# Head sums in two float32r products, with their buffers in the spare columns up to the inverse

## The chip, the cores and the metric

The kernel runs on one NeuronCore of one Trainium2 chip. The metric is the device time of one execution in microseconds (us); lower is better.

## The reference, cut to what matters

A two-layer decoder trunk on x of 512 tokens by 1024 features. Layer 0 mixes tokens by RWKV-7 (8 heads of 64, a state updated along the tokens) and by stick-breaking attention (8 heads of 64); layer 1 by a gated linear recurrence; each is followed by a mixture of 16 experts. The change touches layer 0 only, where four quantities are summed over the 64 features of a head:

```python
kk = heads(k * k_k)
kk = kk / jnp.maximum(jnp.sqrt(jnp.sum(kk * kk, axis=-1, keepdims=True)), 1e-12)
...
bonus = jnp.sum(r_h * k_h * r_k.astype(f32), axis=-1, keepdims=True) * v_h
...
q = rmsnorm(heads(p[..., :B_WIDTH]), q_norm_g)
k = rmsnorm(heads(p[..., B_WIDTH:2 * B_WIDTH]), k_norm_g)
```

The state recurrence is computed in chunks of 64 tokens; that needs the inverse of a triangular 64 by 64 matrix for each head and chunk, before any step of the recurrence.

## The kernel before, in words

Features lie on the 128 partitions and tokens along the free axis, so two heads (a pair) share a tile of 128x512, and a sum over a head's 64 features is a matrix product with a 128x128 matrix of ones in two diagonal blocks: `bo` (ones) and `bo64` (ones divided by 64). Both are float32, as is the operand. All large products instead use float32r operands, cut into a rounded high part and a remainder (`split`: a copy on ScalarE, L297, and a subtraction on VectorE, L298), with three products for a full one (L325 to L327).

Layer 0 runs in this order. `lora` makes the decays. `pair(p)`, four times, projects k, r and v of two heads (three projections of 24 products each, `shifted` and `proj_fm`; L338 and L339 take the result out of PSUM), sums over heads twice (the product on L435, used by L436; the one on L450, used by L451) and builds the chunk operands; `chunks` multiplies them (L483, masked on L489; L493 transposes). `qkv(p)`, four times, projects q, k and v of the attention; q and k are squared (L695), summed over heads (L697) and normalised (L698, L699 on ScalarE, L700 on VectorE, which also frees the projection's bank); v is transposed (L709). Then `inverse` inverts the 32x32 diagonal blocks of all chunks at once on VectorE: a transpose (L507) into `Z`, a ladder of 31 multiply and reduce pairs (L513, L514) that read `Z`, two transposes back (L515, and L520 into `TT`), and copies on ScalarE (L517). Small TensorE products complete the 64x64 inverse (L531, L540, taken out on L533 and L542). `values` prepares the values (L562 to L582). After that the recurrence steps and the attention run interleaved in an order written out by hand (z, a1, a2, a3, d1 and so on of `attend`; p1 to a4 of `step`), then the output projection and the experts.

Outside the hand-ordered part, each engine's order is set when the kernel is built, from the program's order and from when operands are expected to be ready. An engine works through its own list in that order, and waits at the head of it.

There are two projection banks in PSUM (`pj`), so a projection can start when the result of the one before last has been taken out. Memory on chip is handed out by an arena of columns; a request takes the free stretch with the least room that fits, and an address reused is waited for:

```python
fit = [(min(o + s, hi) - max(o, lo), max(o, lo)) for o, s in self.free_list]
fit = [f for f in fit if f[0] >= n]
...
return self.take(min(fit)[1], n)
```

Beside the main tile A of 38336 columns there is a spare stretch of 2560 columns (tile S, `self.more`), float32 in layer 0, which `swap` remakes as float32r or float32 later by closing its pool and opening another in the same place.

Of the kernel before, what the change touches and what calls it, by code (L numbers as in the profile page):

```python
# [8 lines left out]
F32 = mybir.dt.float32  # L9
F32R = mybir.dt.float32r  # L10
# [8 lines left out]
T = 512  # L19
D = 1024  # L20
# [13 lines left out]
SCOLS = 2560  # L34
# [2 lines left out]
P0, P1 = 7, 7  # L37
LOW = 6584
MID = LOW + 3 * 2048
WO0 = [LOW + D * i for i in range(5)] + [20152 + D * i for i in range(3)]  # L40
WO1 = LOW + 7056
FLY = 5
QQ = 3
# [116 lines left out]
class Kern:  # L160
# [180 lines left out]
    def consts_even(self):  # L341
        nc, ar = self.nc, self.ar

        self.bo = ar.get(128)
        self.bo64 = ar.get(128)
        for b, v in ((self.bo, 1.0), (self.bo64, 1.0 / 64)):
            nc.gpsimd.memset(b.f(), 0.0)
            for s in range(2):
                nc.gpsimd.memset(b.f()[s * 64:s * 64 + 64, s * 64:s * 64 + 64], v)

        self.cm = ar.get(128)
        nc.gpsimd.memset(self.cm.f(), 1.0)
        for s in range(2):
            v = self.cm.f()[s * 64:s * 64 + 64]
            nc.gpsimd.affine_select(v[:, 0:64], v[:, 0:64], [[1, 64]], OP.is_gt, 0.0, base=0, channel_multiplier=-1)
            nc.gpsimd.affine_select(v[:, 64:128], v[:, 64:128], [[1, 64]], OP.is_ge, 0.0, base=0, channel_multiplier=-1)

        self.atc = ar.get(128)
        self.identb, self.late = self.atc.b(2, 128)[:, 0], self.atc.b(2, 128)[:, 1]
        nc.gpsimd.tensor_copy(self.identb, self.ident)  # L360
        nc.gpsimd.memset(self.late, 0.0)
        nc.gpsimd.affine_select(self.late, self.late, [[-1, 128]], OP.is_gt, -FAR, base=0, channel_multiplier=1)

        self.sm = ar.get(T)
        nc.gpsimd.memset(self.sm.f(), 1.0)
        nc.gpsimd.memset(self.sm.f(8, 64)[:, :, 0:1], 0.0)

    def lora(self):
        nc, ar, I = self.nc, self.ar, self.I
        self.L1, self.G1, self.G2 = ar.get(T), ar.get(T), ar.get(T)  # L370

        du = ar.get(T)
        dv, q = du.f(), [slice(s * 64, s * 64 + 64) for s in range(2)]
        for s, name in enumerate(("decay_up", "iclr_up")):
            nc.sync.dma_start(dv[q[s]], I[name][0])
        sig = []
        self.shifted(LORA, self.L1.f())
        sig.append(nc.scalar.activation(self.L1.f()[0:64], self.L1.f()[0:64], AF.Tanh))
        self.shifted(1664, self.G1.f())
        sig.append(nc.scalar.activation(self.G1.f(), self.G1.f(), AF.Sigmoid))  # L380
        self.shifted(1696, self.G2.f())
        sig.append(nc.scalar.activation(self.G2.f(), self.G2.f(), AF.Sigmoid))
        self.SG, self.AA = ar.get(4 * T), ar.get(4 * T)
        for p in range(4):
            z = [self.bank("rw") for _ in q]
            for s in range(2):
                nc.tensor.matmul(z[s], dv[q[s], p * 128:p * 128 + 128], self.L1.f()[q[s]], start=True, stop=True)
            for b, dst, name in zip(z, (self.SG, self.AA), ("w0", "a0")):
                sig.append(nc.scalar.activation(dst.f(4, T)[:, p], b, AF.Sigmoid, bias=self.v(name, p)))
        du.free()  # L390
        self.L1.free()
        self.switch(sig)
# [11 lines left out]
    def after(self, ins):  # L404
# [2 lines left out]
            mybir.DependencyClass.NoSync, mybir.DependencyReason.DATA), reason="table set order")  # L407
        return ins

    def pair(self, p):  # L410

        nc, ar = self.nc, self.ar
        r, k, v = ar.get(T), ar.get(T), self.VF.f(4, 64 + T)[:, p, 64:]
        nc.gpsimd.memset(self.VF.f(4, 64 + T)[:, p, 0:64], 0.0)
        self.shifted(512 + p * 128, k.f())
        self.shifted(p * 128, r.f())
        self.shifted(1024 + p * 128, v)
        if p:
            self.products()
        sg, aa = self.SG.f(4, T)[:, p], self.AA.f(4, T)[:, p]  # L420

        c = ar.get(T)
        nc.vector.tensor_tensor_scan(c.f(), self.sm.f(), sg, 0.0, OP.mult, OP.add)
        lam, li = ar.get(8 * 65), ar.get(T)
        L = lam.f(8, 65)
        nc.gpsimd.memset(L[:, :, 0:1], 1.0)
        self.after(nc.scalar.activation(L[:, :, 1:65], c.f(8, 64), AF.Exp, scale=-KAPPA))
        self.after(nc.scalar.activation(li.f(), c.f(), AF.Exp, scale=KAPPA))
        c.free()
        nc.gpsimd.tensor_copy(self.LC.f(4, 8)[:, p], L[:, :, 64:65])  # L430

        sq = ar.get(T)
        nc.scalar.activation(sq.f(), k.f(), AF.Square, scale=self.v("k_k", p))
        b = self.bank("rw")
        nc.tensor.matmul(b, self.bo.f(), sq.f(), start=True, stop=True)  # L435
        nc.vector.tensor_scalar(sq.f(), b, 1e-24, 65536.0, OP.max, OP.mult)  # L436
        self.after(nc.scalar.activation(sq.f(), sq.f(), AF.Ln))
        self.after(nc.scalar.activation(sq.f(), sq.f(), AF.Exp, scale=-0.5))
        kk = ar.get(T)
        nc.vector.scalar_tensor_tensor(kk.f(), k.f(), self.kk256(p), sq.f(), OP.mult, OP.mult)  # L440
        sq.free()
        km = ar.get(T)
        nc.vector.tensor_scalar(km.f(), aa, -1.0, self.v("k_a", p), OP.add, OP.mult)
        nc.vector.scalar_tensor_tensor(km.f(), km.f(), 1.0, k.f(), OP.add, OP.mult)
        k.free()

        bp = ar.get(T)
        nc.vector.scalar_tensor_tensor(bp.f(), r.f(), self.v("r_k", p), km.f(), OP.mult, OP.mult)
        b = self.bank("rw")
        nc.tensor.matmul(b, self.bo.f(), bp.f(), start=True, stop=True)  # L450
        nc.vector.tensor_tensor(self.BV.f(4, T)[:, p], b, v, OP.mult)  # L451
        nc.gpsimd.tensor_scalar(self.BV.f(4, T)[:, p], self.BV.f(4, T)[:, p], self.v("gn_b", p), None, OP.add)
        bp.free()

        AR = self.AR.f(4, 8, 3, 64)[:, p]
        for s in range(2):
            q, o = slice(s * 64, s * 64 + 64), slice(64 - s * 64, 128 - s * 64)
            nc.gpsimd.memset(AR[o, :, s], 0.0)
            nc.vector.scalar_tensor_tensor(AR[q, :, s], L[q, :, 0:64], -1.0, kk.f(8, 64)[q], OP.mult, OP.mult)
        nc.vector.tensor_tensor(AR[:, :, 2], L[:, :, 1:65], r.f(8, 64), OP.mult)  # L460
        r.free()
        lam.free()
        BK = ar.get(8 * 128)
        bk = BK.f(8, 2, 64)
        nc.gpsimd.tensor_tensor(kk.f(), kk.f(), aa, OP.mult)
        for s in range(2):
            q = slice(s * 64, s * 64 + 64)
            nc.gpsimd.tensor_tensor(bk[q, :, s], kk.f(8, 64)[q], li.f(8, 64)[q], OP.mult)
            nc.vector.tensor_tensor(bk[q, :, 1 - s], km.f(8, 64)[q], li.f(8, 64)[q], OP.mult)
        kk.free()  # L470
        km.free()
        li.free()
        self.products = lambda: self.chunks(p, AR, BK)
# [212 lines left out]
    def qkv(self, p):  # L686

        nc, ar = self.nc, self.ar
        w = self.I["w_in_even"][0]
        for i, g in ((0, self.qg8), (1, self.v("k_norm_g"))):  # L690
            b = self.proj_fm(w, A_COLS + i * 512 + p * 128, 128)
            if not p and i:
                self.products()
            sq = self.scr.next().f()[:, 0:T]
            nc.scalar.activation(sq, b, AF.Square)  # L695
            m = self.bank("at")
            nc.tensor.matmul(m, self.bo64.f(), sq, start=True, stop=True)  # L697
            self.after(nc.scalar.activation(sq, m, AF.Ln, bias=self.eps[:, 0:1]))  # L698
            self.after(nc.scalar.activation(sq, sq, AF.Exp, scale=-0.5))  # L699
            nc.vector.scalar_tensor_tensor(self.QK[p].f(2, T)[:, i], b, g, sq, OP.mult, OP.mult)  # L700
# [206 lines left out]
    def even(self):  # L907
# [2 lines left out]
        self.columns()  # L910
        self.consts_even()
        self.scr.free()
        self.scr = Ring(ar, 3, T)
        self.X.free()
        self.lora()
        self.VF, self.BV = ar.get(4 * (64 + T)), ar.get(4 * T)
# [6 lines left out]
            b.free()  # L923
        self.route_in()
        self.QZ = ar.get(256, 4096)
        self.VT, self.QK = [[ar.get(n) for _ in range(4)] for n in (T, 2 * T)]
        for p in range(4):
            self.qkv(p)
        self.cm.free()
        self.inverse()  # L930
        self.UV = ar.get(8 * 4 * 128)
# [27 lines left out]
        nc.sync.dma_start(gu[96:128, 1], I["gate_up"][0, 128:160])  # L959
        self.out_w(I["w_out_even"][0], self.ks)  # L960
        self.a_out()
        for b in (self.AR, self.BV, self.G1, self.G2, self.gup, self.scr, self.bo, self.bo64):
            b.free()

    def even_out(self):
# [654 lines left out]
    def run(self):  # L1620
        tc, nc = self.tc, self.nc
        with ExitStack() as ctx:
# [8 lines left out]
            self.YD = [self.dr.tile([T, D], F32, name=f"YD{l}") for l in range(2)]  # L1631
            self.constants()
            self.sw = ctx.enter_context(ExitStack())
            self.more = self.swap(F32)
            self.scr = Ring(ar, 4, D)
            self.whi = Ring(rr, 2, D)
            self.wlo = Ring(rr, 2, D)
            self.even()
            self.more = ar.take(self.more, SCOLS)
            self.even_out()  # L1640
            self.moe(0)
            self.odd()
# [34 lines left out]
```

## Time and profile before

| what | value |
|---|---|
| median of 3 runs | 1229.35 us (1228.08 to 1234.36) |
| the profiled execution's own time | 1228.33 us |
| its span, first to last instruction | 1226.6 us |
| busy TensorE (PE) / VectorE (DVE) / ScalarE (ACT) / GpSimd (POOL) | 95% / 80% / 66% / 39% |
| mean granted TensorE clock | 0.984 |

All times below are us from the span's start. PE is TensorE's product, PEld its weight load, which overlaps. A float32 product appears as two instructions with one line number, a float32r product as one. The stages of layer 0 that matter here lie between 40 and 240 us.

### The profile page before, as it was taken

How to read it: one execution, taken by the hardware profiler on the slowest of the kernel's cores; microseconds unless marked ns; L12 is line 12 of the kernel's file. 1: busy time of each engine (PE TensorE's matmuls, PEld its weight loads, DVE VectorE, ACT ScalarE, POOL GpSimd, SP SyncE). 2: the span in 40 equal slices, each digit the busy share in tenths (PEclk: the TensorE clock that was granted, in tenths of full speed). 3: DMA queues.
4: the chain of work that ended last, by engine and by line, in shares of the span. 5: the costliest groups of instructions: out<-in, count | busy, mean ns of one | idle time of the engine just before them, and what ended most of it. 6: DMA issues, size and time to landing. Idle time of an engine off the chain costs nothing. (4 is left out here: it accounts for less than half of the span.)

```text
span 1226.6 us, 18324 instructions
## 1 busy us (share of the span) xinstructions
PE 1160.2 (95%) x6782; PEld 855.5 (70%) x6783; DVE 986.5 (80%) x1279; ACT 807.0 (66%) x1077; POOL 483.7 (39%) x319
## 2 busy tenths in 40 slices
PE   7999999899997899999999999999988999999997
PEld 6777776776675677777776766777766777777764
DVE  4387796577768799999998565697667999999986
ACT  6533545587536688888887564756436888888883
POOL 9043200210021367667765011300113566666753
PEclk9999999899998999999999999999998999999999
DMA  6312221016867899999993622276578999999974
GB/s 173 86 52 69 69 69 35 2 37 212 297 240 269 293 349 366 358 351 351 350 361 107 187 69 68 70 238 242 203 237 299 349 362 361 352 345 342 349 237 149
DMA packets 152390, 274.47 MB, mean 224 GB/s; under 512 B 8171, under 2 KB 59052, under 8 KB 152294
## 3 DMA queue, kind: packets, MB, share of 16 engines
q1 hardware_dynamic: 142438, 247.85, 58.5%
q0 software_dynamic: 7840, 18.04, 6.3%
q10 hardware_dynamic: 2016, 7.34, 1.5%
q8 instruction: 55, 0.90, 0.3%
q14 instruction: 41, 0.34, 0.1%
HBM read 258.80 MB, written 22.28 MB: 229 GB/s over the span
## 5 line engine op out<-in xcount | busy, mean ns | idle before, releaser
L297 ACT ACTIVATE R<-A 128x1024 fp32r<-128x1024 f32 (+1 forms) x451 | 473.1, 1053 | 193.1 <-PE ps_pj L1353 65.6
L298 DVE TENSOR_TENSOR R<-A,R 128x1024 fp32r<-128x1024 f32 (+1 forms) x362 | 494.1, 1398 | 82.8 <-ACT R L297 78.7
L298 POOL TENSOR_TENSOR R<-A,R 128x1024 fp32r<-128x1024 f32 x89 | 255.1, 2866 | 237.1 <-ACT R L297 232.8
L1354 PE MATMUL ps_pj<-R 128*96 128x512 f32 x512 | 205.6, 402 | 9.9 <-DVE R L298 9.9
L1352 PE MATMUL ps_pj<-R 128*96 128x512 f32 x512 | 206.2, 403 | 0.0
L1353 PE MATMUL ps_pj<-R 128*96 128x512 f32 x512 | 204.1, 399 | 0.0
L327 PE MATMUL ps_pj<-R 128*128 128x512 f32 x296 | 118.3, 400 | 3.5 <-DVE R L298 3.5
L325 PE MATMUL ps_pj<-R 128*128 128x512 f32 x296 | 119.4, 403 | 1.5 <-DVE A L700 0.6
L326 PE MATMUL ps_pj<-R 128*128 128x512 f32 x296 | 119.4, 403 | 0.0
L1354 PEld LDWEIGHTS ps_pj<-R 128*96 128x96 f32 x512 | 84.1, 164 | 47.0 <-DVE R L298 10.9
L1353 PEld LDWEIGHTS ps_pj<-R 128*96 128x96 f32 x512 | 84.4, 165 | 35.5 <-DVE R L298 0.3
L1379 PE MATMUL ps_at<-R 128*96 128x512 f32 x256 | 103.7, 407 | 5.0 <-PEq L1574 1.9
L1352 PEld LDWEIGHTS ps_pj<-R 128*96 128x96 f32 x512 | 84.5, 165 | 33.9 <-issue 0.5
L1381 PE MATMUL ps_at<-R 128*96 128x512 f32 x256 | 101.5, 396 | 0.0
L1380 PE MATMUL ps_at<-R 128*96 128x512 f32 x256 | 101.4, 396 | 0.0
L327 PEld LDWEIGHTS ps_pj<-R 128*128 128x128 f32 x296 | 55.6, 188 | 20.0 <-DVE R L298 5.7
L1388 POOL DMA_INDIRECT YD<-A x30 | 67.3, 2243 | 4.8 <-issue 2.4
L325 PEld LDWEIGHTS ps_pj<-R 128*128 128x128 f32 x296 | 55.6, 188 | 19.2 <-issue 3.4
L1155 POOL TENSOR_TENSOR A<-A 128x1024 f32<-128x1024 f32 x6 | 16.2, 2719 | 126.8 <-DVE A L861 87.2
L326 PEld LDWEIGHTS ps_pj<-R 128*128 128x128 f32 x296 | 55.6, 188 | 14.3 <-issue 3.6
L298 DVE TENSOR_TENSOR R<-ps_rw,R 128x384 fp32r<-128x384 f32 x92 | 47.7, 542 | 12.7 <-ACT R L297 12.6
L1257 DVE TENSOR_TENSOR A<-A 128x384 bf16<-128x384 f32 x32 | 57.8, 1817 | 0.0
(443 smaller groups left out, 1987.0 us busy)
## 6 DMA issues: line engine op xcount, KB each, us to landing
A<-in_exp_w_up_dram SPq DMA_DIRECT2D x61, 1024.0 KB
A<-in_exp_w_down_dram SPq DMA_DIRECT2D x61, 1024.0 KB
A<-in_exp_w_gate_dram SPq DMA_DIRECT2D x59, 1024.0 KB
A<-in_w_in_even_dram SPq DMA_DIRECT2D x27, 512.0 KB
A<-in_w_in_odd_dram SPq DMA_DIRECT2D x20, 512.0 KB
S<-in_exp_w_gate_dram SPq DMA_DIRECT2D x5, 1024.0 KB
A<-in_w_out_odd_dram SPq DMA_DIRECT2D x10, 512.0 KB
A<-in_x_dram SPq DMA_DIRECT2D x8, 512.0 KB
```

The lines of the kernel that those rows point to most:

```text
L297: a = self.nc.scalar.activation(hi, src, AF.Copy)
L298: return a, (eng or self.nc.vector).tensor_tensor(lo, src, hi.bitcast(F32), OP.subtract)
L325: nc.tensor.matmul(p[0:n], hi[:, k], Hh[:, k], start=k == 0, stop=False)
L326: nc.tensor.matmul(p[0:n], hi[:, k], Hl[:, k], start=False, stop=False)
L327: nc.tensor.matmul(p[0:n], lo[:, k], Hh[:, k], start=False, stop=k == KD - 1)
L1352: self.nc.tensor.matmul(b, xh[:, k], hi, start=k == 0, stop=False)
L1353: self.nc.tensor.matmul(b, xl[:, k], hi, start=False, stop=False)
L1354: self.nc.tensor.matmul(b, xh[:, k], lo, start=False, stop=k == KD - 1)
L1379: nc.tensor.matmul(yb[n], hh[:, k], hi[:, cs], start=k == 0, stop=False)
L1380: nc.tensor.matmul(yb[n], hl[:, k], hi[:, cs], start=False, stop=False)
L1381: nc.tensor.matmul(yb[n], hh[:, k], lo[:, cs], start=False, stop=k == 3)
L1388: self.nc.gpsimd.indirect_dma_start(out=self.YD[l][:, :], out_offset=bass.IndirectOffsetOnAxis(ap=ix[0:SL], axis=0), in_=y.rearrange("p a ...
```

## The change

The two matrices of ones get float32r copies, made on GpSimd. Each of the sums on L435, L450 and L697 (16 in all) no longer multiplies its float32 operand directly. A new helper, `head_sum`, cuts the operand into a high part and a remainder in a buffer of 1024 float32r columns, `hs`, shared by all sums, and adds two float32r products. The sums in `a_out` stay float32.

To hold the copies and `hs`, half of the spare columns (1280 of 2560) becomes a float32r tile, with an arena of its own (`self.sums`). After the last `qkv` its pool is closed, and a float32 tile of the same 1280 columns (`self.rest`) is opened in its place and added to the main arena, ahead of `inverse`. At the end of layer 0's mixing both halves are dropped and the whole spare stretch is remade. As 1280 columns fewer are there meanwhile, some buffers are placed by hand (`scr`, `L1`, `G1`, `G2`, the output weights), and the fourth `QK` buffer is asked for one `qkv` later.

```diff
-WO0 = [LOW + D * i for i in range(5)] + [20152 + D * i for i in range(3)]
+WO0 = [LOW + D * i for i in range(6)] + [21176 + D * i for i in range(2)]
@@ consts_even
-        self.bo = ar.get(128)
-        self.bo64 = ar.get(128)
-        for b, v in ((self.bo, 1.0), (self.bo64, 1.0 / 64)):
+        bo, self.bo64 = ar.get(128), ar.get(128)
+        self.bo, self.bo64r, self.hs = [self.sums.get(n) for n in (128, 128, 2 * T)]
+        for b, v in ((bo, 1.0), (self.bo64, 1.0 / 64)):
...
+        for a, b in ((self.bo, bo), (self.bo64r, self.bo64)):
+            nc.gpsimd.tensor_copy(a.r(), b.f())
+        bo.free()
@@ lora
-        self.L1, self.G1, self.G2 = ar.get(T), ar.get(T), ar.get(T)
+        self.L1, self.G1, self.G2 = ar.get(T, 0, 65536), ar.get(T, 65536), ar.get(T, 65536)
@@
+    def head_sum(self, out, w, src):
+
+        hi, lo = self.hs.r(T), self.hs.r(T, off=T)
+        self.split(hi, lo, src)
+        self.nc.tensor.matmul(out, w.r(), hi, start=True, stop=False)
+        self.nc.tensor.matmul(out, w.r(), lo, start=False, stop=True)
@@ pair
-        nc.tensor.matmul(b, self.bo.f(), sq.f(), start=True, stop=True)
+        self.head_sum(b, self.bo, sq.f())
...
-        nc.tensor.matmul(b, self.bo.f(), bp.f(), start=True, stop=True)
+        self.head_sum(b, self.bo, bp.f())
@@ qkv
-            nc.tensor.matmul(m, self.bo64.f(), sq, start=True, stop=True)
+            self.head_sum(m, self.bo64r, sq)
@@ even
-        self.scr = Ring(ar, 3, T)
+        self.scr = Ring(ar, 3, T, 0, LOW)
...
-        self.VT, self.QK = [[ar.get(n) for _ in range(4)] for n in (T, 2 * T)]
+        self.VT, self.QK = [[ar.get(n) for _ in range(m)] for n, m in ((T, 4), (2 * T, 3))]
         for p in range(4):
+            if p == 1:
+
+                self.QK.append(ar.get(2 * T))
             self.qkv(p)
+        self.sw1.close()
+        n = 2 * T + 256
+        self.rest = ar.add(self.sw1.enter_context(self.tc.tile_pool(name="sw2", bufs=1)).tile([128, n], F32, name="S1"), n)
         self.cm.free()
         self.inverse()
...
-        for b in (self.AR, self.BV, self.G1, self.G2, self.gup, self.scr, self.bo, self.bo64):
+        for b in (self.AR, self.BV, self.G1, self.G2, self.gup, self.scr, self.bo64):
@@ run
-            self.more = self.swap(F32)
+
+            n, self.sums = 2 * T + 256, Arena()
+            self.more = ar.add(self.sw.enter_context(tc.tile_pool(name="sw0", bufs=1)).tile([128, SCOLS - n], F32, name="S0"), SCOLS - n)
+            self.sw1 = ctx.enter_context(ExitStack())
+            self.sums.add(self.sw1.enter_context(tc.tile_pool(name="sw1", bufs=1)).tile([128, n], F32R, name="S1r"), n)
...
-            self.more = ar.take(self.more, SCOLS)
+            ar.drop(self.more, SCOLS - n)
+            ar.drop(self.rest, n)
+            self.sw1.close()
+            self.more = ar.take(self.swap(F32), SCOLS)
```

## Rows read from the trace of the kernel before

**Rows 1.** The page: busy time of each engine over the whole span.
```profile
PE 1160.2 (95%) x6782; PEld 855.5 (70%) x6783; DVE 986.5 (80%) x1279; ACT 807.0 (66%) x1077; POOL 483.7 (39%) x319
```

**Rows 2.** Windows of 30 us; columns as the first line says.
```profile
core 0: us, PE busy (x) PEld busy (x) DVE busy (x) ACT busy (x) POOL busy (x), PEclk, DMA share, GB/s
...
90.00:120.00 30.00, 28.66 (x138) 21.14 (x136) 24.64 (x32) 9.02 (x13) 13.52 (x12) 1.00 0.20 53
...
180.00:210.00 30.00, 28.07 (x114) 20.10 (x113) 23.72 (x23) 15.55 (x21) 1.40 (x1) 1.00 0.16 43
```

**Rows 3.** Groups of PE by line, 40 to 225 us: busy, mean ns, idle before.
```profile
L325 PE MATMUL ps_pj<-R 128*128 128x512 f32 x190 | 77.0, 405 | 1.2 <-DVE A L700 0.6 <-DVE S L339 0.4
...
L697 PE MATMUL ps_at<-A 128*128 128x512 f32 x16 | 8.8, 629 | 1.5 <-ACT A L695 1.5
```

**Rows 4.** Timeline of PE around one sum: start, duration, engine, line, operation.
```profile
161.17 0.39 PE L325 MATMUL ps_pj<-R 128*128 128x512 f32 x1
161.40 1.11 PE L697 MATMUL ps_at<-A 128*128 128x512 f32 x2
161.95 0.80 PE L326 MATMUL ps_pj<-R 128*128 128x512 f32 x1
162.58 0.39 PE L327 MATMUL ps_pj<-R 128*128 128x512 f32 x1
```

**Rows 5.** Timeline of ACT around the same sum, idle before in brackets.
```profile
160.75 0.58 ACT L695 ACTIVATE A<-ps_pj 128x512 f32<-128x512 f32 x1
162.55 0.69 ACT L698 ACTIVATE A<-ps_at,A 128x512 f32<-128x512 f32 x1 [1.22 <-PE ps_at L697]
163.27 0.63 ACT L699 ACTIVATE A<-A 128x512 f32<-128x512 f32 x1
```

**Rows 6.** Timeline of DVE in one pair, around its second sum.
```profile
88.47 3.45 DVE L469 TENSOR_TENSOR A<-S,A 64x512 f32<-64x512 f32 x2
91.95 0.69 DVE L451 TENSOR_TENSOR A<-ps_rw,A 128x512 f32<-128x512 f32 x1
92.56 0.74 DVE L339 SCALAR_TENSOR_TENSOR S<-ps_pj,A 128x512 f32<-128x512 f32 x1
```

**Rows 7.** DVE groups, 150 to 215 us: busy, mean ns, idle before.
```profile
L513 DVE TENSOR_TENSOR A<-A 128x1 f32<-128x1 f32 (+30 forms) x31 | 15.8, 509 | 0.9
L514 DVE TENSOR_REDUCE A<-A 128x1 f32<-128x1 f32 (+30 forms) x31 | 15.6, 504 | 0.9
...
L700 DVE SCALAR_TENSOR_TENSOR A<-ps_pj,A 128x512 f32<-128x512 f32 x7 | 5.2, 747 | 8.3 <-ACT A L699 8.3
```

**Rows 8.** Timeline of DVE, the transposes around the ladder.
```profile
153.07 2.10 DVE L507 STREAM_TRANSPOSE A<-A 128x1024 f32<-128x1024 f32 x1 [2.47 <-ACT A L506]
...
198.01 2.23 DVE L515 STREAM_TRANSPOSE A<-A 128x1024 f32<-128x1024 f32 x1
200.13 1.93 DVE L520 STREAM_TRANSPOSE A<-A 128x1024 f32<-128x1024 f32 x1
```

**Rows 9.** Timeline of all engines, 201 to 230 us.
```profile
201.87 1.12 PE L697 MATMUL ps_at<-A 128*128 128x512 f32 x2 [1.53 <-ACT A L695]
...
208.37 0.58 ACT L695 ACTIVATE A<-ps_pj 128x512 f32<-128x512 f32 x1
...
213.95 3.02 PE L531 MATMUL ps_rw<-A 32*32 32x32 f32 x96
...
216.90 1.13 PE L752 MATMUL ps_pj<-A 128*128 128x256 f32 x4
...
219.43 4.67 PE L540 MATMUL ps_rw<-A 32*32 32x32 f32 x125
...
229.61 0.95 DVE L565 COPY A<-ps_rw 64x192 f32<-64x192 f32 x3 [1.60 <-ACT A L563]
```

**Rows 10.** Window of 5 us, columns as in Rows 2.
```profile
220.00:225.00 5.00, 5.00 (x117) 4.93 (x115) 1.38 (x2) 1.36 (x3) 1.80 (x1) 0.69 0.01 3
```

**Rows 11.** Groups of PE, 215 to 241 us, columns as in Rows 3.
```profile
L562 PE MATMUL ps_rw<-A 128*128 128x128 f32 x32 | 5.6, 341 | 0.8 <-DVE A L565 0.8
```

## The prediction

> **What bounds the kernel now.** I read the page first, then windows of 30 us through layer 0's mixing, and there the groups by line, the waits and the timeline of each engine. PE is busy 95% of the span [rows 1]. In the stage that the change touches it is busy 28 to 29 us of every 30, and the other engines have room: DVE 24 us, ACT 9 to 16 us [rows 2]. So from 40 to 210 us the pace is PE's, and a microsecond taken from PE is worth nearly one as long as nothing makes PE wait. The reader is to see a second thing there: in the last part of that stage, 153 to 202 us, DVE works through the inverse's ladder while PE is still on the projections of `qkv` [rows 7, 8]. The ladder is long, and it costs nothing now: it ends at 202.06 (200.13 plus 1.93), while PE first asks for its product `TT` on L531 at 213.95 [rows 8, 9]. After that come small products, copies and steps that each wait for the one before; nothing there is spare.
>
> **What a sum costs on PE.** A float32 sum starts at 161.40, and two products later PE is at 162.58; less one usual pitch of 0.23 (161.17 to 161.40) that is 0.95 us for the sum [rows 4]. Two float32r products at that pitch are 0.46. The saving is 0.49 us for each of 16 sums, 7.8 us at most. Against it each sum gets a copy on ACT and a subtraction on DVE of 128x512. The nearest rows are 0.58 us (L695, [rows 5]) and 0.69 us (L451, [rows 6]), so the operand is ready about 1.4 us later with the handovers, and DVE and ACT get 11 and 9 us more work in all.
>
> *Pairs (8 sums).* Around the second sum DVE runs without a gap: L469 for 3.45, L451, L339, and PE waits for that L339, 0.4 us in the stage [rows 3, 6]. A subtraction of 0.69 more in this chain, against 0.49 less on PE ahead of it, is a wash: 0.2 us worse for a pair if DVE sets the pace, 1.0 better if PE does. By the second the eight save 3.9; by the first, and with the other subtraction late too, they lose up to 3. I take 0, as the row shows DVE last. The early products of a pair have time: their square is there long before their bank.
>
> *`qkv` (8 sums).* The chain from a projection's end to its bank is L695, sum, L698, L699, L700: 0.58, 0.46, 0.69, 0.63, 0.75 with about 0.15 of handover each [rows 5, 7], and now 1.4 more, near 5.3 us. The bank is wanted after the next projection, 24 products of 0.23 and a sum, 6.0 us. It is hidden, if DVE is at hand; if not, 0.5 us a sum is lost. So seven sums before the last give 7 x 0.49 = 3.4.
>
> **The buffer, which decides.** I followed the arena's requests in their order. Before, when `inverse` asks for `Z` (1024 columns), the tightest stretch is one of 1032 in the main tile, given back by the last pair, so L507 can start at 153. After, that stretch went to the fourth `QK`. What is left with room is 4224 columns at the bottom and the 1280 of `rest`, and the arena takes the smaller: `Z` lies in `rest`, and `TT` after it. But `rest` has the addresses of `hs`, which the head sums use up to k of the last `qkv`. L507 writes `Z`, so it must wait for the last sum's products, and behind it waits the whole ladder, as every step reads `Z`. What hid the ladder, the projections of `qkv`, is then past: only v of the last pair is left.
>
> When is the last sum done? Its square starts at 208.37 [rows 9]: 0.58, then 1.4 for the two parts, 0.46 for the products and 0.2 to be seen: 211.0 at the old pace. Less 3.4 from the earlier sums, and less 2.1 for waits of PE that the ladder itself caused and that go with it (1.5 on L695, held on ACT behind L517, and 0.6 on L700, held on DVE among L513 and L514) [rows 3, 9]: 205.5.
>
> Then the chain on DVE: L507 2.1; the ladder 15.8 + 15.6 busy and 0.9 + 0.9 idle [rows 7], 33.2; L515 at 2.1 to the next start; L520 1.9 [rows 8]; one L700 in between, 0.7. That is 40.0, and `TT` is there at 245.5, where PE began L531 at 213.95: **31.5 us later**. Nothing else can go in meanwhile in quantity: the steps need the inverse and stand early in the hand order on all three engines.
>
> Three small things follow. Products of 1.5 us (L752 and L709, from 216.90 to the second L531 at 218.40) stand between the L531 now [rows 9]; they will be past: -1.5. Likewise the first attention unit's ACT work, for which L565 now waits 1.60 us [rows 9], can be done in the pause: -1.0. And PE will have stood still for some 30 us. The granted clock already falls there now, to 0.69 of full in 220 to 225, the 1.2 GHz level for most of it, though PE shows no gap; 125 products L540 take 4.67 us, 37 ns each, and 96 of L531 at the full clock 3.02, 31 ns each [rows 9, 10]. The 128 of L531 at the slower pace cost +0.7.
>
> The Trainium skill ("TensorE: Matmul & The Clock Gate", Part 1) says that the half clock is the idle state, and sustained products lift it. By it L540's first products would begin slow too, 6 ns each on up to 128, so at most 0.8 us would come on top. The trace agrees only in part: its clock falls while PE is busy with small products, and no row of before shows a pause as long as this one.
>
> Sum: 31.5 - 1.5 - 1.0 + 0.7 = 29.7 us from the first step of the recurrence on. Everything behind, the expert weights' loads too, starts from buffers that this stage frees, so it shifts as a whole: 1228.3 + 29.7 = **1258 us**. The sum is made against the profiled execution's 1228.33, which is 1.0 under the median. The other edits cost nothing that I can find: the output weights land in buffers freed at the same places, the spare stretch is remade after `a_out`, whose gates held it before too, and the GpSimd copies run ahead of 40 us. If the remake came late, the expert load waiting for it would hold those behind it on SP's queue, some 1 us.
>
> **The rivals.**
> *The ladder stays hidden* (it ends on the other side: faster). If `Z` got other columns, or L507 could start before the last sum, only the sums would count: between 3.9 (`qkv` alone) and 7.8, and DVE's extra 5.5 us under the ladder lie inside the 11.9 between 202.06 and 213.95 [rows 8, 9]. Time about 1223. It decides from where `Z` is written: before about 170 nothing is lost. Against it: the smallest stretch is chosen without regard to time, and reused addresses are waited for. Chance 0.04.
> *The pause is partly filled, and the pairs gain.* The transposes of `values` do not need the inverse; if they move ahead (5.6 us busy and 0.8 of waits on L562, [rows 11]), and the pairs give 3.9, the time is 1258 - 6.4 - 3.9 = 1247.7. Against the first: their destination shares columns with the ladder's scratch. Chance 0.13, with all between 1247 and 1252.
> *The pause costs more.* The pairs lose 3, each of seven sums of `qkv` 0.5, the slow clock the 0.7 once more: 1258 + 3 + 3.5 + 0.7 = 1265.2. Chance 0.13, above 1264.
> *Cancelled.* Gain and pause meet within 0.5% (6 us, about what a measurement of this kernel can tell from no change): 0.03. It would take a pause of 8 us, a fifth of the ladder.
>
> **How the numbers follow.** The forecast, 1252 to 1264 by its own unknowns, has 0.67. The range 1248 to 1266 takes in most of the two neighbours and leaves out 0.04 + 0.03 and their far ends, together under 0.2. Faster 0.04, same 0.03, slower 0.93.
>
> **What would show it.** In the profile after: L507 starting near 205, at the end of the last sum's second product and released by it; L513 and L514 in one unbroken run on DVE with PE idle for some 30 us, and a granted clock near half there; sums of 0.46 us on PE; no 1.5 us wait before the last q sum. I am wrong if L507 still starts near 150, if the `qkv` stage gets longer through waits on L298 or L700, or if work of `values` fills the pause.

## The result, and the profile after

The changed kernel takes 1281.48 us (1279.08 to 1283.54) beside 1229.3 for the kernel before: 1.0414 times [1.0393, 1.0435], 52 us slower. I forecast 1258 (1248 to 1266). The sign and the mechanism of the pause came true, the size did not: the time lies 15 us above the range. The profiled span grew from 1226.6 to 1279.1.

The page first: busy time has hardly changed [rows 1]. PE did 3 us more, so the 52 us are nearly all waiting. DVE did 18.4 us more, where 16 subtractions at the 0.69 that I had taken would be 11.

```profile
PE 1163.3 (91%) x6782; PEld 862.4 (67%) x6783; DVE 1004.9 (79%) x1295; ACT 818.0 (64%) x1093; POOL 487.6 (38%) x321
```

Windows of the changed kernel show where (columns as in Rows 2; the first and third are to be held against [rows 2], the last against [rows 10], and the second against this line of the kernel before):

```profile
120.00:150.00 30.00, 29.32 (x162) 22.21 (x161) 23.13 (x36) 15.19 (x23) 8.25 (x12) 1.00 0.34 88
```

```profile
90.00:120.00 30.00, 26.27 (x124) 19.72 (x124) 23.00 (x30) 11.09 (x17) 8.94 (x12) 0.94 0.19 53
120.00:150.00 30.00, 25.66 (x121) 19.23 (x120) 23.15 (x30) 10.31 (x15) 8.76 (x7) 0.94 0.20 52
180.00:210.00 30.00, 29.86 (x133) 23.52 (x132) 10.25 (x11) 14.22 (x22) 0.00 (x0) 1.00 0.27 71
...
230.00:240.00 10.00, 0.00 (x0) 0.00 (x0) 9.24 (x23) 0.00 (x0) 0.00 (x0) 0.50 0.00 0
...
270.00:275.00 5.00, 5.00 (x109) 5.00 (x107) 0.69 (x1) 3.25 (x6) 1.01 (x1) 0.50 0.01 3
```

There are two places. While the pairs run, PE is busy 2.4 and 3.7 us less in 30 than before, and its mean granted clock is 0.94 in place of 1.00. From 230 on PE does nothing while DVE alone works: the forecast pause. Between them, in `qkv`, PE is fuller than before.

**The pause.** DVE's timeline around the last head sum (L298 subtracts the remainder, L418 is its product, L517 the ladder's transpose, L523 and L524 its steps, L525 and L530 the transposes back; they answer to [rows 7, 8]):

```profile
212.18 0.69 DVE L298 TENSOR_TENSOR S1r<-A,S1r 128x512 fp32r<-128x512 f32 x1
...
218.40 1.84 DVE L298 TENSOR_TENSOR S1r<-A,S1r 128x512 fp32r<-128x512 f32 x1 [2.60 <-ACT S1r L297]
220.83 2.10 DVE L517 STREAM_TRANSPOSE S<-A 128x1024 f32<-128x1024 f32 x1 [0.59 <-PE ps_at L418]
...
225.08 2.27 DVE L523 TENSOR_TENSOR A<-A,S 128x25 f32<-128x25 f32 x1
227.38 0.18 DVE L524 TENSOR_REDUCE A<-A 128x5 f32<-128x25 f32 x1
...
259.14 2.01 DVE L525 STREAM_TRANSPOSE A<-A 128x1024 f32<-128x1024 f32 x1
261.06 1.89 DVE L530 STREAM_TRANSPOSE S<-A 128x1024 f32<-128x1024 f32 x1
```

L517 writes to tile S, the spare columns, where it wrote to A before, and is released by L418, the last product that reads `hs`: as forecast, `Z` lies where `hs` lay, and the ladder waits for the last sum. `TT` is there at 262.95, and PE (first the waits, then its timeline) stood 37.4 us for it, where before `TT` was there 11.9 us ahead of L531 [rows 8, 9]:

```profile
PE ps_rw L541 <- DVE S L530: 37.4, 1, 37.4
```

```profile
263.09 6.28 PE L541 MATMUL ps_rw<-S,A 32*32 32x32 f32 x125 [37.41 <-DVE S L530]
...
269.32 6.29 PE L550 MATMUL ps_rw<-A 32*32 32x32 f32 x125
```

**The pairs.** PE's timeline at the second sum of a pair (L417 is the product of the high part, L418 that of the remainder), then DVE's and POOL's:

```profile
92.41 0.40 PE L327 MATMUL ps_pj<-R 128*128 128x512 f32 x1
95.76 0.50 PE L418 MATMUL ps_rw<-S1r 128*128 128x512 f32 x1 [2.96 <-DVE S1r L298]
...
97.61 0.63 PE L327 MATMUL ps_pj<-R 128*128 128x512 f32 x1
98.04 0.63 PE L325 MATMUL ps_pj<-R 128*128 128x512 f32 x1
```

```profile
90.57 3.46 DVE L479 TENSOR_TENSOR A<-A 64x512 f32<-64x512 f32 x2
94.06 1.64 DVE L298 TENSOR_TENSOR S1r<-A,S1r 128x512 fp32r<-128x512 f32 x1
```

```profile
91.88 3.28 POOL L478 TENSOR_TENSOR A<-A 64x512 f32<-64x512 f32 x2
```

PE stands at the head of its list for a remainder that DVE has listed behind L479, and that then takes 1.64 us rather than the 0.69 at 212.18. After the wait some of the products come every 0.43 us (97.61 to 98.04), about half of the usual pace of 0.23, for some 2.5 us. L479 itself is slow: its two operations take 1.73 each, while one of the same shape takes 0.69 in the run E6 below, begun when no operation of GpSimd was under way:

```profile
94.80 0.69 DVE L479 TENSOR_TENSOR A<-A 64x512 f32<-64x512 f32 x1
```

So the price of sharing with GpSimd stood already in the 3.45 of [rows 6]: there GpSimd ran L465 and L468 from 87.85 to 93.07. A pair took 24.5 us before (first sum taken out at 58.0 in the first pair and at 131.4 in the fourth) and takes 28.3 now (55.7 and 140.6).

### The profile page after: what moved, and what is told of

Its sections match the earlier page's. It is cut to its first block, busy times and chain, and to the rows that moved or that the text cites. A ratio compares the mean times of both kernels' runs of the same rounds, so it can differ in the third digit from the quotient of the medians.

```text
span 1279.1 us, 18374 instructions
## 1 busy us (share of the span) xinstructions
PE 1163.3 (91%) x6782; PEld 862.4 (67%) x6783; DVE 1004.9 (79%) x1295; ACT 818.0 (64%) x1093; POOL 487.6 (38%) x321
## 5 line engine op out<-in xcount | busy, mean ns | idle before, releaser
L298 DVE TENSOR_TENSOR R<-A,R 128x1024 fp32r<-128x1024 f32 (+1 forms) x362 | 494.2, 1398 | 105.8 <-ACT R L297 96.7
L298 POOL TENSOR_TENSOR R<-A,R 128x1024 fp32r<-128x1024 f32 x89 | 258.8, 2907 | 218.9 <-ACT R L297 216.2
L327 PEld LDWEIGHTS ps_pj<-R 128*128 128x128 f32 x296 | 56.9, 192 | 15.9 <-DVE R L298 3.1
L325 PEld LDWEIGHTS ps_pj<-R 128*128 128x128 f32 x296 | 56.7, 192 | 15.1 <-issue 2.2
L326 PEld LDWEIGHTS ps_pj<-R 128*128 128x128 f32 x296 | 56.8, 192 | 12.3 <-issue 0.7
L298 DVE TENSOR_TENSOR R<-ps_rw,R 128x384 fp32r<-128x384 f32 x92 | 47.8, 543 | 15.2 <-ACT R L297 15.0
```

What stands on the lines that cost most here:

```text
L298: return a, (eng or self.nc.vector).tensor_tensor(lo, src, hi.bitcast(F32), OP.subtract)
L325: nc.tensor.matmul(p[0:n], hi[:, k], Hh[:, k], start=k == 0, stop=False)
L326: nc.tensor.matmul(p[0:n], hi[:, k], Hl[:, k], start=False, stop=False)
L327: nc.tensor.matmul(p[0:n], lo[:, k], Hh[:, k], start=False, stop=k == KD - 1)
```

## The experiments

E2 is an edit of the kernel before; the others are edits of the changed kernel. Each kernel computes the whole result. The edits are excerpts. Each ratio is to runs of the kernel before on the same chip (medians 1228.7 to 1229.4).

**E1, Z apart.** `Z`, the other two buffers beside it, `TT` and `W` come from the main tile, so the ladder shares no column with `hs`.

```diff
-        Z, XT, tmp = [ar.get(1024) for _ in range(3)]
+        Z, XT, tmp = [ar.get(1024, 0, 65536) for _ in range(3)]
-        TT = ar.get(1024)
+        TT = ar.get(1024, 0, 65536)
-        W = ar.get(1024)
+        W = ar.get(1024, 0, 65536)
```

> The changed kernel, with Z, TT and W of the inverse asked from the main tile alone, so that no column of the head sums' buffer is written by the ladder. Theory A (two causes: the ladder pushed behind the last sum, and the wait of TensorE for the second sum of each pair): the ladder goes back under the projections, the pairs stay slow (9.2 us late at the last pair's first sum, some 3 more by the end of the attention's projections), so 1229 + 12 = 1241 us, 1236 to 1246. Theory B (the cuts on VectorE and ScalarE cost all of it, the place of Z little): above 1270 us. Theory C (the place of Z is all of it, and the sums gain as forecast): 1222 to 1226 us.

Measured 1242.25, 1.0102 [1.0079, 1.0125]: 39.2 of the 52.2 us are gone by the place of the buffers alone. DVE's timeline shows the ladder among `qkv` again, with weight cuts between its steps:

```profile
169.53 2.07 DVE L517 STREAM_TRANSPOSE A<-A 128x1024 f32<-128x1024 f32 x1 [0.33 <-ACT A L516]
171.53 1.18 DVE L298 TENSOR_TENSOR R<-A,R 128x1024 fp32r<-128x1024 f32 x1
...
222.01 2.02 DVE L530 STREAM_TRANSPOSE A<-A 128x1024 f32<-128x1024 f32 x1
```

It ends at 224.03, and PE reaches L541 at 227.1: hidden, by 3 us. But 13 us stay that my prediction didn't have.

**E2, the wait alone.** The kernel before, its sums float32 and its buffers in place, with one wait added: the ladder's transpose waits for the last float32 head sum.

```diff
-            nc.tensor.matmul(m, self.bo64.f(), sq, start=True, stop=True)
+            self.sum = nc.tensor.matmul(m, self.bo64.f(), sq, start=True, stop=True)
...
-        nc.vector.transpose(z, tmp.f(32, 32).rearrange("p c i -> p i c"))
+        t = nc.vector.transpose(z, tmp.f(32, 32).rearrange("p c i -> p i c"))
+        self.tc.add_manual_dep(t.ins, self.sum.ins.name, ...)
```

> The kernel before, float32 sums and all, with one wait added: the transpose ahead of the ladder waits for the product of the last head sum. Theory A: the last sum ends near 208, the chain on VectorE takes 42 us as in the changed kernel, so TT is there at 250, 36 us later than TensorE asked for it before, and 3 us more go to the slow clock after the pause: 1229 + 39 = 1268 us, 1262 to 1273. Theory B: under 1240 us.

Measured 1264.96, 1.0287 [1.027, 1.0304]: the wait by itself costs 36 us. Its transpose starts at 207.13, and the waits of PE are like those of the changed kernel:

```profile
PE ps_rw L533 <- DVE A L522: 36.0, 1, 36.0
```

E1 and E2 bracket the pause from both sides, 39 us taken out and 36 us put in. The other 13 are cuts or layout.

**E3, pairs alone; E4, q and k alone.** Both with `Z` apart. E3 cuts the eight sums of the pairs, E4 the eight of `qkv`; the others are float32 products, in E4 with a float32 `bo` that is kept.

```diff
 # E3
-            self.head_sum(m, self.bo64r, sq)
+            nc.tensor.matmul(m, self.bo64.f(), sq, start=True, stop=True)
 # E4
-        self.head_sum(b, self.bo, sq.f())
+        nc.tensor.matmul(b, self.bof.f(), sq.f(), start=True, stop=True)
-        self.head_sum(b, self.bo, bp.f())
+        nc.tensor.matmul(b, self.bof.f(), bp.f(), start=True, stop=True)
```

> As the run with Z apart, but only the sums of the state pairs in two float32r products; those of q and k float32 as before. Theory A: TensorE waits 3 us at the second sum of each pair, and the pairs are 9 us late at the last one: 1236 to 1242 us. Theory C (a pair is a wash or gains): 1225 to 1231 us.

> As the run with Z apart, but only the sums of q and k in two float32r products; those of the state pairs float32 as before. Theory A: eight sums save 0.49 us each on TensorE and nothing waits for their cuts: 1229.3 - 3.9 = 1225.4 us, 1224 to 1228. Theory B (each cut costs where it stands): 1231 to 1236 us.

E3 gave 1242.73, 1.011 [1.0093, 1.0128], 0.7 above the upper end of what I expected. E4 gave 1240.74, 1.0084 [1.0067, 1.0102], where I expected a gain: a miss. Each half alone costs nearly as much as both, so the halves do not add, and I looked for something common to both. In E4 the chunk products of a pair (L493) come right behind the second sum, and wait there; PE's timeline:

```profile
91.73 1.13 PE L460 MATMUL ps_rw<-A 128*128 128x512 f32 x2 [0.72 <-DVE A L458]
95.70 1.57 PE L493 MATMUL ps_rw<-A 64*128 64x128 f32 x6 [2.85 <-DVE A L479]
...
148.41 0.50 PE L417 MATMUL ps_at<-S1r 128*128 128x512 f32 x1 [0.46 <-ACT S1r L297]
...
157.80 0.78 PE L418 MATMUL ps_at<-S1r 128*128 128x512 f32 x1
```

The last two rows are a cost of the cuts in `qkv` themselves: the two products of the first cut k sum stand 9.4 us apart, with the last pair's chunk products between them on PE's list, and L710 takes that k out at 162.42, for 154.94 in E5. Against the layout alone (E5, next) E4 is 8.0 us slower, 3.6 of it by the first small product (222.41 against 218.81); what the other 4.4 hang on is not shown (see the last section).

**E5, layout alone.** Both edits at once, `Z` apart: the other buffers are asked for as the change does, `bo` is kept, and no sum is cut.

> As the run with Z apart, but every sum a float32 product as before: the two halves of the spare columns, the moved buffers and the GpSimd copies stay, the cuts go. Theory D (the moved buffers change the order in which each engine's list is written, and that order costs the pairs some 8 us, whatever the sums do): 1235 to 1241 us, the products of a pair's chunks standing on TensorE's list right behind a second sum, and waiting there. Theory A (the cuts alone make the pairs slow): 1228 to 1231 us.

Measured 1232.76, 1.0033 [1.0015, 1.0052], between the two theories: the layout by itself costs 3.5 us, which I had put at nothing. PE's written order is another one: before, the chunk products (L483) came a stretch of projections after the second sum (L450); here they stand next to the sum and wait 2.85 for L479, as in E4 (95.43 in E5). PE's timeline of the kernel before:

```profile
88.60 1.13 PE L450 MATMUL ps_rw<-S,A 128*128 128x512 f32 x2 [0.25 <-DVE S L448]
...
99.70 2.05 PE L483 MATMUL ps_rw<-A 64*128 64x128 f32 x24
```

**E6, remainder first.** E1, with the two products of L479 ordered behind the remainder on DVE.

```diff
-        self.split(hi, lo, src)
+        self.cutting = self.split(hi, lo, src)[1]
...
-            nc.vector.tensor_tensor(bk[q, :, 1 - s], km.f(8, 64)[q], li.f(8, 64)[q], OP.mult)
+            self.behind(nc.vector.tensor_tensor(bk[q, :, 1 - s], km.f(8, 64)[q], li.f(8, 64)[q], OP.mult), self.cutting)
```

> As the run with Z apart, all 16 sums cut, but the two products on VectorE that follow in a pair are listed behind the subtraction that makes the remainder of the second sum. Theory A (TensorE waits 3 us a pair for that subtraction, because it is listed behind 3.45 us of other work, and loses 1.5 us more to the lower clock after the wait): 1242 less 3 x 4.4 = 1229 us, 1227 to 1235. Theory D (the order of the rest of the pair sets its pace): 1238 to 1243 us.

Measured 1237.19, 1.0062 [1.0043, 1.008], between the two theories: 5.1 us better than E1, and only part of what I expected. DVE's timeline, then PE's:

```profile
88.53 2.30 DVE L298 TENSOR_TENSOR R<-A,R 128x1024 fp32r<-128x1024 f32 x1
90.75 1.75 DVE L298 TENSOR_TENSOR S1r<-A,S1r 128x512 fp32r<-128x512 f32 x1
92.42 1.75 DVE L479 TENSOR_TENSOR A<-A 64x512 f32<-64x512 f32 x1
```

```profile
92.55 0.80 PE L418 MATMUL ps_rw<-S1r 128*128 128x512 f32 x1 [1.79 <-DVE S1r L298]
```

The remainder is first of the two, and still slow, behind a weight cut that is slow too (2.30; 1.18 in E1 at 171.53): GpSimd ran L475 from 87.91 to 89.74 and L478 from 89.83 to 93.63. PE's wait fell from about 3 to 1.79. The fourth pair's second sum is taken out at 147.77, for 155.36 in E1 and 146.76 in E5. The first small product starts at 218.9, as in E5 (218.8), 8.2 before E1.

**E7, a busy pause.** The changed kernel with 160 products on PE during the pause, into a bank that nothing reads, to see what PE's rest costs behind it. They are useless work, added.

```diff
+        warm, Hh = self.bank("o"), self.HTh.r(KD, T)
+        for i in range(160):
+            m = nc.tensor.matmul(warm, Hh[:, i % KD, 0:128], Hh[:, i % KD], start=True, stop=True)
+            if not i:
+                self.behind(m, self.sum)
```

> The changed kernel as it is, with 160 products of no use on TensorE behind the last head sum, in a bank that is free then, so that TensorE does not stand still while VectorE works through the ladder. If the clock at 0.50 after the pause costs what the two groups of small products took longer (6.3 us each against some 4.5), the time falls by 3 to 4 us, to 1278. If the small products are set by something else, it stays at 1281 to 1282; if the extra products run past TT it rises.

Measured 1283.14, 1.0431 [1.0407, 1.0454]: the hoped-for gain did not come. Windows around the end of the pause, then PE's timeline:

```profile
230.00:260.00 30.00, 30.00 (x134) 24.73 (x132) 28.52 (x44) 0.00 (x0) 0.00 (x0) 1.00 0.00 1
260.00:265.00 5.00, 2.11 (x66) 1.89 (x66) 3.00 (x2) 3.70 (x4) 0.00 (x0) 1.00 0.01 3
265.00:270.00 5.00, 5.00 (x85) 4.29 (x82) 0.00 (x0) 2.46 (x5) 0.28 (x1) 0.51 0.00 0
270.00:275.00 5.00, 5.00 (x109) 5.00 (x107) 0.69 (x1) 1.56 (x3) 0.76 (x1) 0.50 0.02 3
```

```profile
263.14 3.65 PE L546 MATMUL ps_rw<-S,A 32*32 32x32 f32 x96 [2.89 <-DVE S L535]
266.72 1.22 PE L767 MATMUL ps_pj<-A 128*128 128x256 f32 x2
...
269.57 6.29 PE L555 MATMUL ps_rw<-A 32*32 32x32 f32 x125
```

The granted clock stayed at its upper level through the pause, and fell within a few us of the small products' start. PE still stood 2.89 us before them. The first 96 were faster (3.65, 38 ns each; 50 in the changed kernel), but two products of L767 now stand among them, and the second 125 took 6.29 us as in the changed kernel. So the run does not price the pace after the pause cleanly.

**E8 to E10, whether a mended version beats the kernel before.** All with `Z` apart. E8 cuts only the four first sums of the pairs. E9 cuts twelve of sixteen (the second sums float32), and lists each pair's chunk products behind the projection of v. E10 is E5 with that order.

```diff
 # E8, E9
-        self.head_sum(b, self.bo, bp.f())
+        nc.tensor.matmul(b, self.bof.f(), bp.f(), start=True, stop=True)
 # E8
-            self.head_sum(m, self.bo64r, sq)
+            nc.tensor.matmul(m, self.bo64.f(), sq, start=True, stop=True)
 # E9, E10
-                    nc.tensor.matmul(b[:, i * 128:i * 128 + 128], BK.f(8, 128)[q, g * 4 + i],
-                                     AR[q, g * 4 + i, s:3:2 - s], start=True, stop=True)
+                    self.behind(nc.tensor.matmul(...), self.plast)
```

> The changed layout with Z apart; only the first sum of each state pair (4 sums) in two float32r products, the second sums and those of q and k float32. Theory A (of the pairs' cuts it is the second one that costs, as TensorE reaches its remainder before VectorE has made it; the first has seven microseconds to spare): the layout alone gave 1232.8, less 4 x 0.49 = 1231 us, 1229 to 1233. Theory B (every cut costs where it stands): 1236 us or more.

> As the run with first sums alone, the sums of q and k cut too (12 of 16), and the products of a pair's chunks listed behind the projection of v on TensorE, as in the kernel before. If nothing waits for these cuts, the layout alone in that order (about 1230) less 12 x 0.49 = 1224 us, 1222 to 1227, faster than both kernels. Theory E (the cuts of q and k lie among the ladder's steps on VectorE, which lengthens the ladder until it ends after the projections): 1230 to 1238 us, with TT after the v projection of the last pair.

> The layout alone, every sum float32, with the products of a pair's chunks listed behind the projection of v on TensorE. Theory D (what the layout costs is the wait of 2.85 us at the chunks' products that stand too early on the list, once, and the clock it takes down): 1232.8 - 2.8 = 1230 us, 1228 to 1231. If the layout costs in another way: 1232 to 1234 us.

E8: 1234.2, 1.0036 [1.0019, 1.0053], 1.2 above the upper end of what I expected and the same as the layout alone, so four cut sums gain nothing that can be measured. E9: 1237.65, 1.0082 [1.0052, 1.0112], slower than before. Its time lies where the second theory put it, but by luck: that theory wanted `TT` after the last v projection, and `TT` is there at 220.71, before that projection's last product at 223.44. The chunk products stand between the two products of a k sum instead, as in E4 (149.68 and 159.19). E10: 1234.18, 1.0038 [1.0025, 1.0051], a miss: the wait went elsewhere, as PE's timeline shows.

```profile
92.59 1.12 PE L460 MATMUL ps_rw<-A 128*128 128x512 f32 x2 [0.70 <-DVE A L458]
99.11 0.77 PE L325 MATMUL ps_pj<-R 128*128 128x512 f32 x1 [5.40 <-DVE A L339]
```

With the chunk products gone from behind the sum, the next projection waits longer, for the bank that L339 takes out, on the same DVE; E9 has the same wait of 5.4 us. No version beats the kernel before.

## Why the prediction was wrong

The account by medians, from one kernel to the next: 1229.3 before; 1232.8 with the layout (+3.5, E5); 1242.3 with all sums cut (+9.5, E1); 1281.5 with `Z` over `hs` (+39.2). By the first small product in the profiles: 213.95, 218.8, 227.1, 263.09, that is +4.9, +8.3 and +36.0. In the terms of my sum, the profiles' 52.5 stand against 29.7, and the 22.8 between them are about these: the last sum is 15.3 us later than forecast, the chain on DVE 2.1 longer, the small terms 3.9 worse, and 1.2 lie behind the first step's copy.

*The buffer* is right. `Z` is in `rest`, L517 is released by the last sum, the ladder runs in one piece with PE idle beside it, and nothing of `values` filled the pause; E1 and E2 bear out both the mechanism and, at 39 and 36 us, that it is nearly the whole ladder. The rival in which the ladder stays hidden is refuted; of the one in which the pause costs more, the direction came true, 16 us beyond its own sum.

*"I take 0" for the pairs* is the step that failed, with what hangs on it, the last sum at 205.5. The bound that I kept was a loss of up to 3; the pairs' sums alone cost some 10 over the layout (E3 against E5) and all sums 9.5, in place of the 3.4 that I had them gain, and E6 gives back 5.1 by DVE's order in the pairs alone. I had added 0.69 for a subtraction to DVE's chain, 0.2 us a pair at worst. The list has it behind L479 (3.46), and beside POOL it takes 1.64, so PE stands for 3 us a pair. I had seen DVE without a gap there [rows 6], and priced the new instruction, not the queue ahead of it. The cost of the half clock behind each wait I had left out.

*"The other edits cost nothing that I can find"* failed too: 3.5 us in E5. I had looked for waits on addresses and remakes, and not at the order of the lists, which changed with the buffers. That the order is what costs is argued, not shown: E10 moved the chunk products and gained nothing. Together these two made the last sum late: its product ended before 220.83, not at 205.5, and 13.7 later than in E2 (207.13), which has neither.

*The gain in `qkv`* I had at 3.4 for the sums and 2.1 for the ladder's waits. From one k to the next it is 18.4 us (L710 at 184.44 and 202.87) for 19.4 before (172.33 and 191.71). But E2, whose sums are float32, has 18.8 (170.91 and 189.73): most of that gain is the ladder's absence, and in E4 and E9 the cuts in `qkv` cost time.

*The chain on DVE* was 42.1 (220.83 to 262.95) for 40.0. The groups of DVE hold the excess in L523, 17.9 us for 15.8 [rows 7]:

```profile
L523 DVE TENSOR_TENSOR A<-A,S 128x1 f32<-128x1 f32 (+30 forms) x31 | 17.9, 576 | 1.1
L524 DVE TENSOR_REDUCE A<-A 128x1 f32<-128x1 f32 (+30 forms) x31 | 15.6, 504 | 1.0
```

One step of 128x25 took 2.27 instead of about 0.18; POOL's timeline has the reason:

```profile
224.97 2.34 POOL L298 TENSOR_TENSOR R<-A,R 128x1024 fp32r<-128x1024 f32 x1
```

*The small terms* went the other way. I had −1.8 for what follows the pause; from the first small product to the first step's copy it took 27.6 us (263.09 to 290.72) for 25.5, so +2.1. The mis-sized one is the slow pace. I had read it as 37 ns from a stretch with a mean granted clock of 0.69, part of which ran at the upper level; at 0.50 throughout, 125 products take 6.28 and 6.29, 50 ns each. For both groups of 128 that is some 4 us in place of 0.7 (an estimate from these rows). The wait put at 1.0 gave back 0.2: from the first product of `values` to L587 it took 7.4 us (275.54 to 282.95), for 7.6 before (224.03 to 231.68).

The Trainium skill ("TensorE: Matmul & The Clock Gate", Part 1), by which at most 0.8 would have come on top for a start from rest, does not cover that. The trace agrees that the clock is at 0.50 in the rest (230 to 240), but the second group is as slow in E7, where PE had worked until 2.89 us before the first.

Three things stay open. Why the moved buffers change the lists, and whether that is what costs the 3.5, was not traced. The 4.4 us between E6 and E5 lie behind the first small product, which starts at the same time in both; the next section shows what differs there, not why. And a cut that keeps the old layout was not run.

## What to carry to other kernels

A buffer that a stage shares with the last use of the stage before it ties the two in time: ask of each reuse what else in the program is hidden only because it starts early. When an operand gets one more preparation step, price the engine's list ahead of that step and the neighbour beside it, not the instruction alone. A change of the memory plan is to be timed by itself, with the arithmetic as it was; here that was 3.5 us, as much as I had expected all sums of `qkv` to gain.

## What the runs showed of the hardware

**An operation of DVE with two operands in SBUF stands still while GpSimd runs one there that began before it.** L523, a multiplication, began at 225.08 and ended at 227.35, GpSimd's ran from 224.97 to 227.31; the last remainder, begun at 218.40, ended at 220.24, 0.5 after GpSimd's operation of 217.31:

```profile
217.31 2.39 POOL L298 TENSOR_TENSOR R<-A,R 128x1024 fp32r<-128x1024 f32 x1 [56.27 <-ACT R L297]
```

This is what the Trainium skill says ("SBUF — State Buffer", Summary: rules for kernel authors): of a VectorE operation with two inputs in SBUF and a GpSimd one that reads SBUF, the second to issue blocks until the first is done. The trace agrees. The subtraction took 0.69 alone and 1.64, 1.75 and 1.84 us beside GpSimd for 128x512, and 1.2 and 2.30 for 128x1024.

**The granted clock falls during the small products without a pause ahead of them too, and the moment differs.** Windows of E6 and of E5 from the first small product on, at 218.9 and 218.8, with PE at work before it in both:

```profile
219.00:224.00 5.00, 5.00 (x108) 4.31 (x108) 0.75 (x1) 3.73 (x7) 0.16 (x1) 0.79 0.01 3
224.00:229.00 5.00, 5.00 (x109) 5.00 (x107) 0.31 (x1) 2.43 (x4) 1.72 (x2) 0.50 0.02 3
```

```profile
219.00:224.00 5.00, 5.00 (x127) 4.64 (x125) 0.00 (x0) 3.60 (x6) 2.92 (x3) 1.00 0.01 3
224.00:229.00 5.00, 5.00 (x146) 4.94 (x143) 1.21 (x2) 1.74 (x3) 1.80 (x1) 0.85 0.02 3
```

From there to the first step's copy it is 29.0 us in E6 and 24.7 in E5. So a few us of a profile's time lie in that moment, and the comparison of profiles should be made ahead of it. The mean granted clock also differs between executions of one kernel: nine of E5's ten took 1231.5 to 1234.7 us at 0.980 to 0.983, and one took 1241.2 at 0.973. All four of E4 lie at 0.972 to 0.975, and whether its cuts cause that is open.
